# Seven of ten column blocks of the modulation vectors move from the projections to the hgrn heads and the output projection

## The chip, the cores and the metric

The kernel runs on one core of a Trainium2 chip. The metric is device time in microseconds (us) for one execution, the median of several; lower is better. The engines are PE (TensorE; PEld is its weight load), DVE (VectorE), ACT (ScalarE), POOL (GpSimd) and SP, which issues most DMAs. Each engine and each queue works through its instructions strictly in the order in which the program lists them.

## The reference

Two transformer blocks on 1024 tokens of width 1024, all in fp32. The places that bear on the change, cut:

```python
s_lat = jax.nn.silu(c);  s_ctx = jax.nn.silu(c_ctx)            # [1, 1024], [1024]
sh1, sc1, g1, sh2, sc2, g2 = jnp.split(s_lat @ ada_w + ada_b, 6)   # ada_w [1024, 6144]
h = modulate(rmsnorm(x, norm1_g), sh1, sc1);  p = h @ w_in
y_hy = hyena_mixer(p[..., :1536], ...)          # two long convolutions by FFT
y_hg, _ = hgrn_mixer(p[..., 1536:], pc, ...)    # 4 heads, two directions
x = x + g1 * (concat(y_hy, y_hg) @ w_out)
x = x + g2 * ec_moe(modulate(rmsnorm(x, norm2_g), sh2, sc2), ...)
...
# second block, layers 0 and 1, for the latent rows and for 256 context rows
shift, scale, gate = jnp.split(silu(c) @ w_mod[l] + b_mod[l], 3)   # w_mod[l] [1024, 3072]
```

The modulation vectors are the products `silu(c) @ ada_w`, `silu(c) @ w_mod[0]` and `silu(c) @ w_mod[1]`, each also for the context's `c_ctx`: 6, 3 and 3 blocks of 1024 columns. The first two blocks of `ada_w` are wanted at once. The other four are first wanted by the output projection (`g1`) and by the norm behind it (`sh2`, `sc2`), `w_mod[0]` by the second block's context stream, which starts beside the hgrn heads, and `w_mod[1]` by layer 1, a long time after.

## The kernel before

The program is written as pieces of work in a priority order, and a scheduler lays the instructions out on each engine. Tiles come from pools; a tile waits until the slot that it takes is released. The pieces, in order:

1. **Start**: the first two column blocks of `ada_w`, the norm, the transposed rows `T` as high and low halves.
2. **Projections and hyena side by side** (`interleave` in `build`): `hy_proj` and `hg_proj` multiply `T` with weights (`pp` tiles in PSUM, weights `ah`, `al`), while the hyena filters, their spectra and the long convolutions run (`pf` tiles). A third stream, `mods_rest`, lays ten column blocks of modulation vectors between them.
3. **hgrn** (`ctx_state`, `hgrn_head`, `ph` tiles), two heads in flight on tiles marked 0 and 1. Beside the heads stands the part of the second block's context stream that its input alone decides: `ctx_first` and `ctx_side` (`cp` and `cm` tiles, weights `wr` split into `wh` and `wl`). Its last eight pieces are the gate's, one per 128 channels: a 512 KB load, a split by ACT and POOL, 24 matmuls, one store to `dgc`.
4. **Output projection and routing** (`out_proj`: `pp`, `pi`, `pq` tiles, weights `wo`), then `topk` with `ctx_heads` (`cp` again), then the experts and the second block, which the change leaves as they are.

A column block is one step of `mod_rows`. It takes sixteen weight tiles of 128 rows and 512 columns, each with one matmul whose stationary side is the two columns of `silu` (a row of the order; fp32 is run in two passes, so the trace counts two matmuls). The sums lie in four strips of one PSUM tile `mp`. Two bias rows are loaded, four DVE additions (`mr<-mr,mp`) finish the block, and it is stored. After the last block of a group `rows_to_cols` loads part of it back, transposes it on PE and copies it out on ACT.

Of the kernel before, what the change touches and what calls it, by code (L numbers as in the profile page):

```python
# [22 lines left out]
D = 1024  # L23
# [107 lines left out]
class Kern:  # L131
# [11 lines left out]
    # ------------------------------------------------------------ storage  # L143
# [26 lines left out]
    def cst(self, shape, dt=F32, name="c"):  # L170
        return self.pc.tile(list(shape), dt, name=self.nm(name))
# [7 lines left out]
    # ------------------------------------------------------------ operations  # L179
# [73 lines left out]
    def columns(self):  # L253
        """the small vectors, 128 channels to a column"""
# [44 lines left out]
    # ------------------------------------------------------------ modulation vectors  # L299
# [6 lines left out]
    def mod_rows(self, w, bias, c0, ncols, s, rows, pt, tmp, raw):  # L306
        """rows[:, c0:c0+ncols] (DRAM, one row per vector) = s^T w + bias, 1024 columns per step"""
        for b0 in range(c0, c0 + ncols, 1024):
            ps = self.ps(pt)
            for k in range(8):  # L310
                for cb in range(2):
                    r = self.t(raw, [128, 512])
                    self.dma(r, w[k * 128:k * 128 + 128, b0 + cb * 512:b0 + cb * 512 + 512])
                    p0 = 64 * (k % 2) + 32 * cb
                    self.mm(ps[p0:p0 + 2], s[:, k, :], r, k < 2, k > 5)
# [8 lines left out]
    def rows_to_cols(self, rows, c0, nblk, pt, tmp):  # L324
        """[128, 2, nblk]: column form of rows[:, c0:c0 + 128 nblk]"""
# [9 lines left out]
    def mods_rest(self, pt, tmp, raw):  # L335
        """the modulation vectors of block 2 and the rest of block 1's"""
        I = self.I
        oc, occ = self.offb["c_2"], self.offb["c_ctx_2"]
        s = self.silu_cols(self.cb[:, oc:oc + 8], self.cb[:, occ:occ + 8])
        self.m2 = self.dram([2, 2, 3 * D], name="m2")  # L340
        self.A_2, self.sh_2 = [], []
        on = self.offb["norm_g_2"]
        for l in range(2):
            yield from self.mod_rows(I["w_mod_2"][l], I["b_mod_2"][l], 0, 3 * D, s, self.m2[l], pt, tmp, raw)
            mods = self.rows_to_cols(self.m2[l], 0, 16, pt, tmp)
            A = self.cst([128, 2, 8], name="A")
            for i in range(2):
                self.stt(A[:, i], mods[:, i, 8:16], 1.0, self.cb[:, on + l * 8:on + l * 8 + 8], ADD, MUL)
            self.A_2.append(A)
            self.sh_2.append(mods[:, :, 0:8])  # L350
        yield from self.mod_rows(I["ada_w"][0], I["ada_b"][0], 2 * D, 4 * D, self.scol, self.ada, pt, tmp, raw)
# [6 lines left out]
    # ------------------------------------------------------------ norm + modulate + transpose  # L358
# [18 lines left out]
    def transpose_mod(self, xs, A, sh, pt, tmp, emit, dst=None):  # L377
        """for each block k of D: [128, len(xs)*128 tok] = A * x^T + sh"""
# [40 lines left out]
    def wunits(self, w, c0, nc_, eng=None):  # L419
        """columns c0 .. c0+nc_ of w in units of 512 columns of 128 rows: a list of (hi, lo)"""  # L420
# [3 lines left out]
    def proj(self, w, hT, t0, n, pt):  # L424
        """[128 channels, n tokens] in PSUM"""
# [22 lines left out]
    def filter_mlp(self):  # L448
        """self.hst [128, 1024]: hidden features (hi over lo), one column per lag"""
# [31 lines left out]
    def filter_time(self):  # L481
        """even and odd parts of the windowed two-sided filters to DRAM; self.finv: per channel 1/(norm0 norm1)"""
# [60 lines left out]
    def fwd_butterfly(self, xa, xb):  # L543
        """x_a (a=0..7) in xa, xb [128,4,256]; yields (r, y), y [128, 2, 256] = (sum x cos, sum x sin) of pi a r / 8"""
# [78 lines left out]
    def filter_spectra(self):  # L623
        """Hd[o][half][r]: [128 j, 2, 256] = (Re, -Im) of the unnormalised spectrum at 16 j + r"""
# [19 lines left out]
    # ------------------------------------------------------------ long convolution of one half (256 channels)  # L644
# [156 lines left out]
    def hy_proj(self):  # L801
        """short-convolved v, x1, x2 in [token, channel] form to DRAM; x2 carries the filters' norms"""
# [1278 lines left out]
```

## Time and profile before

| what | value |
|---|---|
| runs | 4019.2 us median of 3 (4012.77 to 4020.24) |
| the profiled execution, from its first to its last instruction | 4024.9 us |
| share of the span busy: PE, DVE, ACT, POOL | 92%, 72%, 57%, 32% |
| projections beside the hyena | 115 to 821 us |
| the last long convolution alone | 821 to 893 us on PE |
| hgrn heads and context | 893 to 1157 us |
| output projection | 1157 to 1273 us |
| routing, up to the first experts | 1273 to 1375 us |

The page gives no time of the profiled execution other than its span, which is 5.7 us above the median of the runs. A window's line gives each engine's busy time in that stretch with the number of instructions, then the granted TensorE clock as a share of full speed, the busy share of the 16 DMA engines and what they moved. A busy matmul time counts a matmul from its start to its modelled end; since the next one starts earlier, the distance from start to start is the price of one in a stream.

### The profile page before, as it was taken

Reading aid. Unit: us, or ns where it says so; the run is one execution under the profiler, and the core shown is the slowest. Engines: PE = TensorE matmul, PEld = TensorE weight load, DVE = VectorE, ACT = ScalarE, POOL = GpSimd, SP = SyncE. Lnnn points to the kernel's source line nnn. Section 1 sums busy time; section 2 is a strip of 40 time slices with the busy share of each in tenths; the row PEclk is TensorE's granted clock in tenths of the full one; section 3 lists DMA queues with packets and bytes.
Section 4 is the critical chain, followed back from the end, with each engine's and each line's share of the span. In section 5 each row is a group of like instructions: output and inputs, shape, how many; then the busy total and the mean of one; then the engine's idle time right before and its main releaser. Section 6 shows DMA issues by size and latency. Waiting matters only on the chain. (4 is left out here: it accounts for less than half of the span.)

```text
span 4024.9 us, 54977 instructions
## 1 busy us (share of the span) xinstructions
PE 3685.7 (92%) x18922; PEld 2946.4 (73%) x18922; DVE 2907.8 (72%) x4414; ACT 2310.5 (57%) x3763; POOL 1290.8 (32%) x940
## 2 busy tenths in 40 slices
PE   6999999976887889999999999979999899999989
PEld 2667666646876677778777777768788788878878
DVE  4587767789843788889888888855677744567772
ACT  4433432226534688678777777755566654466662
POOL 3455533336612322311112111001344610143461
PEclk7999999987988999999999999989999999999999
DMA  7778777772345689999999999951311144131133
GB/s 227 227 227 247 229 234 229 221 237 86 95 151 191 188 298 346 342 326 334 356 365 355 368 362 356 343 178 65 117 53 38 49 149 123 59 121 49 40 97 113
DMA packets 538592, 824.41 MB, mean 205 GB/s; under 512 B 39089, under 2 KB 242887, under 8 KB 538312
## 3 DMA queue, kind: packets, MB, share of 16 engines
q1 hardware_dynamic: 511240, 755.75, 55.2%
q0 software_dynamic: 26048, 64.09, 5.8%
q8 instruction: 149, 2.44, 0.3%
q10 hardware_dynamic: 1024, 1.06, 0.1%
q14 instruction: 131, 1.07, 0.1%
HBM read 712.65 MB, written 107.05 MB: 204 GB/s over the span
## 5 line engine op out<-in xcount | busy, mean ns | idle before, releaser
L187 DVE TENSOR_TENSOR el<-er,eh 128x1024 fp32r<-128x1024 f32 x763 | 946.5, 1289 | 114.9 <-ACT eh L184 108.0
L184 ACT ACTIVATE eh<-er 128x1024 fp32r<-128x1024 f32 x768 | 785.4, 1057 | 144.5 <-PE ea L206 93.2
L205 PE MATMUL ea<-el,xh 128*128 128x512 f32 x1024 | 417.5, 408 | 19.1 <-DVE el L187 16.9
L204 PE MATMUL ea<-eh,xh 128*128 128x512 f32 x1024 | 406.3, 400 | 2.5 <-ACT eh L184 2.5
L206 PE MATMUL ea<-eh,xh 128*128 128x512 f32 x1024 | 405.9, 396 | 0.0
L1277 POOL DMA_INDIRECT acc<-yo,idx x16 | 78.0, 4875 | 757.4 <-DVE yo L196 757.4
L1508 DVE TENSOR_SCALAR_CACHE_REDUCE E<-s,rq 128x512 f32<-128x512 f32 (+1 forms) x384 | 239.3, 656 | 48.3 <-PE s L209 32.6
L205 PEld LDWEIGHTS ea<-el,xh 128*128 128x128 f32 x1024 | 193.7, 189 | 86.4 <-DVE el L187 45.3
L181 ACT ACTIVATE E<-E,a 128x1280 f32<-128x1280 f32 x160 | 216.5, 1359 | 53.5 <-DVE a L1512 49.0
L204 PEld LDWEIGHTS ea<-eh,xh 128*128 128x128 f32 x1024 | 193.9, 189 | 49.4 <-ACT eh L184 3.8
L209 PE MATMUL s<-KA,QA 128*128 128x512 f32 (+1 forms) x768 | 202.8, 388 | 27.8 <-DVE E L1508 27.7
L206 PEld LDWEIGHTS ea<-eh,xh 128*128 128x128 f32 x1024 | 194.0, 189 | 39.6
L205 PE MATMUL ey<-el,hh 128*128 128x512 f32 x512 | 205.4, 401 | 5.2 <-DVE el L187 5.2
L204 PE MATMUL ey<-eh,hh 128*128 128x512 f32 x512 | 203.8, 403 | 4.2 <-ACT eh L184 4.2
L209 PE MATMUL mp<-mr,silu 128*2 128x512 f32 x384 | 188.0, 643 | 21.5 <-DMA mr<-in_ada_w_dram 14.1
L206 PE MATMUL ey<-eh,hh 128*128 128x512 f32 x512 | 202.2, 395 | 0.0
L209 PE MATMUL pt<-dg,E 128*128 128x128 f32 x1280 | 184.1, 290 | 10.0 <-DVE a L1515 4.1
L184 ACT ACTIVATE u<-pp 32x512 f32<-32x512 f32 (+2 forms) x212 | 124.2, 586 | 103.8 <-PE pp L206 97.1
L209 PEld LDWEIGHTS pt<-dg,E 128*128 128x128 f32 x1280 | 170.8, 205 | 15.1 <-issue 9.7
L204 PE MATMUL pp<-T,ah 128*128 128x512 f32 x448 | 180.5, 403 | 0.0
L205 PE MATMUL pp<-T,ah 128*128 128x512 f32 x448 | 179.0, 400 | 0.0
L209 PEld LDWEIGHTS s<-KA,QA 128*128 128x128 f32 x768 | 133.2, 201 | 61.8 <-DVE E L1508 44.2
(527 smaller groups left out, 10043.4 us busy)
## 6 DMA issues: line engine op xcount, KB each, us to landing
er<-in_exp_w_dram SPq DMA_DIRECT2D x768, 512.0 KB
wr<-in_w_in_dram SPq DMA_DIRECT2D x60, 512.0 KB
dc<-in_k_dft_dram POOLq DMA_DIRECT2D x72, 384.0 KB, 4.6
mr<-in_ada_w_dram SPq DMA_DIRECT2D x96, 256.0 KB
mr<-in_w_mod_dram SPq DMA_DIRECT2D x96, 256.0 KB
dc<-in_k_dft_dram POOLq DMA_DIRECT2D x72, 256.0 KB, 4.5
ar<-in_w_in_dram SPq DMA_DIRECT2D x64, 256.0 KB
wr<-in_w_out_dram SPq DMA_DIRECT2D x24, 512.0 KB
```

The source lines that it names most:

```text
L181: return self.nc.scalar.activation(out, in_, func, **kw)
L184: return self.nc.scalar.activation(out, in_, AF.Copy)
L187: return (eng or self.nc.vector).tensor_tensor(out, a, b, op=op)
L204: mm(out, lh, rh, start=first, stop=False)
L205: mm(out, lh, rl, start=False, stop=False)
L206: mm(out, ll, rh, start=False, stop=last)
L209: self.nc.tensor.matmul(out, l, r, start=first, stop=last)
L1277: nc.gpsimd.indirect_dma_start(out=self.acc, out_offset=x[0], in_=yo, in_offset=None, compute_op=ADD)
L1508: nc.vector.tensor_scalar(E[:, k0:k1], o, r, None, op0=MUL, op1=ALU.min, accum_out=mx[:, m, j:j + 1] if nc_ > 1 else mc)
```

## The change

`mods_rest` is cut in three. `mods_layer(0)` (three blocks of `w_mod[0]`) stays beside the projections. `mods_tail` (four blocks of `ada_w`) now stands behind the heads in the program and ahead of `ctx_first`; `mods_layer(1)` (three blocks) stands behind `ctx_side`. The moved blocks load 1024 columns at a time, so each load is 512 KB in place of 256 KB and there are 56 loads in place of 112. They share the two `wr` slots with `ctx_side` and have one slot `mr` beside, and they put their sums into the one `cm` bank that the context stream uses too. Loads, matmuls, additions and stores of a block are otherwise the same. The rest of the diff renames the class, drops comments and docstrings, and runs the same program through `run`.

```diff
-    def mod_rows(self, w, bias, c0, ncols, s, rows, pt, tmp, raw):
+    def mod_rows(self, w, bias, c0, ncols, s, rows, pt, tmp, raw, wide=512):
...
                 for cb in range(2):
-                    r = self.t(raw, [128, 512])
-                    self.dma(r, w[k * 128:k * 128 + 128, b0 + cb * 512:b0 + cb * 512 + 512])
+                    if cb * 512 % wide == 0:
+                        r = self.t(raw[k % len(raw)] if wide > 512 else raw, [128, wide])
+                        self.dma(r, w[k * 128:k * 128 + 128, b0 + cb * 512:b0 + cb * 512 + wide])
                     p0 = 64 * (k % 2) + 32 * cb
-                    self.mm(ps[p0:p0 + 2], s[:, k, :], r, k < 2, k > 5)
+                    self.mm(ps[p0:p0 + 2], s[:, k, :], r[:, cb * 512 % wide:cb * 512 % wide + 512], k < 2, k > 5)
...
+        K.mods_first()
...
-                       (0, 11, [(K.mods_rest("mp", "mr", "mr"), 1)]))
+                   (0, 4, [(K.mods_layer(0, "mp", "mr", "mr"), 1)]))
...
             with ExitStack() as e2:
                 K.open_ps(e2, "right", cp=1, cm=1)
+                K.open(e2, "right", mr=1)
+                for _ in K.mods_tail("cm", "cv", ("wr", "wr", "mr"), 1024):
+                    pass
                 K.ctx_first()
                 K.ctx_side()
+                for _ in K.mods_layer(1, "cm", "cv", ("wr", "wr", "mr"), 1024):
+                    pass
```

How the scheduler lays this out on PE, at the three places that matter. First the end of the projections, before: `pp` rows are the projections, `mp<-mr,silu` rows the modulation vectors, `pf` the last long convolution.

```order
L204 MATMUL pp_8394<-T_402,ah_8361 128x512
L205 MATMUL pp_8394<-T_410,ah_8361 128x512
L206 MATMUL pp_8394<-T_402,al_8362 128x512
L209 MATMUL mp_6943<-mr_6986,silu_127 2x512
L209 MATMUL mp_6943<-mr_6989,silu_127 2x512
L204 MATMUL pf_7351<-yh_7343,dc_7347 128x256
L204 MATMUL pf_7429<-yh_7421,dc_7425 128x256
```

The same place with the change:

```order
L204 MATMUL pp_7962<-T_402,ah_7929 128x512
L205 MATMUL pp_7962<-T_410,ah_7929 128x512
L206 MATMUL pp_7962<-T_402,al_7930 128x512
L204 MATMUL pf_6987<-yh_6979,dc_6983 128x256
L204 MATMUL pf_7065<-yh_7057,dc_7061 128x256
```

Counted as the program lists them (the trace shows each as two passes), 142 of this stage's 160 modulation matmuls stood ahead of the last projection matmul and 18 among the 192 matmuls of the last long convolution. With the change 48 are left, all in the first half of the projections. The second place is the first head, before: `ph` rows are hgrn, `cp` and `cm` the context stream.

```order
L209 MATMUL ph_2215_8693<-hi_2205_8672,hi_2210_8682 128x128 x4
L212 MATMUL ph_2193_8636<-ident_116,hw_2184_8587 128x128 x2
L212 MATMUL cm_10291<-ident_116,cu_10286 128x4
L212 MATMUL cp_10340<-ident_116,cx_10319 128x128
L209 MATMUL ph_2218_8707<-hm_2217_8702,hm_2216_8701 128x128 x4
L209 MATMUL ph_2221_8719<-hm_2220_8714,hm_2219_8713 128x128 x4
```

With the change:

```order
L209 MATMUL ph_2074_8261<-hi_2064_8240,hi_2069_8250 128x128 x4
L209 MATMUL cm_9826<-wr_9827,silu_127 2x512 x2
L212 MATMUL ph_2052_8204<-ident_116,hw_2043_8155 128x128 x2
L209 MATMUL cm_9826<-wr_9831,silu_127 2x512 x2
L209 MATMUL cm_9826<-mr_9835,silu_127 2x512 x2
L209 MATMUL ph_2077_8275<-hm_2076_8270,hm_2075_8269 128x128 x4
L209 MATMUL ph_2080_8287<-hm_2079_8282,hm_2078_8281 128x128 x4
```

All 64 matmuls of `mods_tail` now stand between hgrn matmuls, most of them in the heads' first half, and the context's `cp` matmuls come later: before, all 312 stood ahead of the last hgrn matmul, now 192 do, 48 stand between it and the first `pp` matmul of the output projection, and 72 among the `pp` matmuls. There, the third place, PE had only the output projection's own `pp`, `pi` and `pq` matmuls before:

```order
L204 MATMUL pp_11107<-wo_11018,yt_11029 128x512
L212 MATMUL pi_11077<-ident_116,m_2814_11073 128x128 x4
L205 MATMUL pp_11107<-wo_11019,yt_11029 128x512
L206 MATMUL pp_11107<-wo_11018,yt_11031 128x512
L206 MATMUL pp_11135<-wo_10988,yt_11030 128x512
```

With the change:

```order
L206 MATMUL cp_10645<-Tc_10068,wl_10642 128x256
L209 MATMUL cm_10673<-wr_10678,silu_986 2x512 x2
L209 MATMUL cm_10673<-mr_10682,silu_986 2x512 x2
L212 MATMUL pi_10983<-ident_116,m_2762_10979 128x128 x4
L205 MATMUL pp_10999<-wo_10911,yt_10921 128x512
L206 MATMUL pp_10999<-wo_10910,yt_10923 128x512
```

The 48 matmuls of `mods_layer(1)` stand among the 384 `pp` matmuls of the output projection. On SP their loads stand between the loads of the output projection's own operands.

## Rows read from the trace of the kernel before

**Rows 1.** The page's part 1: engine, busy us, share, instructions.

```profile
PE 3685.7 (92%) x18922; PEld 2946.4 (73%) x18922; DVE 2907.8 (72%) x4414; ACT 2310.5 (57%) x3763; POOL 1290.8 (32%) x940
```

**Rows 2.** Windows over the five stretches, all instructions.

```profile
core 0: us, PE busy (x) PEld busy (x) DVE busy (x) ACT busy (x) POOL busy (x), PEclk, DMA share, GB/s
115.00:821.00 706.00, 687.36 (x3289) 469.14 (x3289) 508.65 (x806) 244.39 (x507) 324.28 (x302) 0.99 0.75 231
821.00:893.00 72.00, 51.39 (x230) 31.10 (x226) 61.96 (x126) 19.90 (x37) 22.90 (x36) 0.81 0.74 239
893.00:1157.00 264.00, 196.84 (x1417) 186.85 (x1417) 222.49 (x354) 145.56 (x373) 147.18 (x105) 0.84 0.33 103
1157.00:1273.00 116.00, 108.63 (x547) 91.45 (x548) 39.30 (x71) 49.56 (x118) 19.65 (x15) 0.95 0.43 147
```

**Rows 3.** PE's waits from 115 to 821 us, the three longest.

```profile
PE pf L204 <- ACT yh L184: 5.8, 2, 3.5
PE pp L212 <- DVE u L196: 5.6, 3, 2.3
PE mp L209 <- DMA mr<-in_w_mod_dram: 4.2, 5, 1.2
```

**Rows 4.** The first two windows, instructions of the tile mp alone (PE, PEld, DVE, ACT).

```profile
115.00:821.00 706.00, 142.63 (x288) 12.31 (x290) 21.77 (x32) 0.39 (x2) 0.99 0.75 231
821.00:893.00 72.00, 18.92 (x36) 1.38 (x32) 4.08 (x6) 0.00 (x0) 0.81 0.74 239
```

**Rows 5.** PE in order of time, late in the projections: start us, us, instruction.

```profile
802.77 0.39 PE L206 MATMUL pp<-T,al 128*128 128x512 f32 x1
803.00 0.39 PE L204 MATMUL pp<-T,ah 128*128 128x512 f32 x1
803.23 0.40 PE L205 MATMUL pp<-T,ah 128*128 128x512 f32 x1
803.56 1.02 PE L209 MATMUL mp<-mr,silu 128*2 128x512 f32 x2
804.51 0.50 PE L206 MATMUL pp<-T,al 128*128 128x512 f32 x1
804.85 0.39 PE L204 MATMUL pp<-T,ah 128*128 128x512 f32 x1
```

**Rows 6.** Two windows within the projections, all instructions.

```profile
250.00:300.00 50.00, 47.98 (x218) 32.33 (x216) 43.01 (x63) 21.07 (x46) 29.80 (x29) 1.00 0.74 218
700.00:750.00 50.00, 50.00 (x207) 31.29 (x206) 42.79 (x67) 14.36 (x28) 29.18 (x18) 1.00 0.76 246
```

**Rows 7.** PE's longest wait for the loads from 821 to 893 us, then PE in order of time.

```profile
PE mp L209 <- DMA mr<-in_ada_w_dram: 4.9, 6, 1.3
896.37 0.31 PE L212 MATMUL mp<-ident,mr 32*128 32x32 f32 x1 [4.02 <-DVE mr L187]
900.54 0.80 PE L209 MATMUL ph<-hw,h 128*128 128x128 f32 x2 [3.86 <-DMA hw<-dVc]
```

**Rows 8.** SP's queue in order of time, same place.

```profile
893.78 0.78 SPq L177 DMA_DIRECT2D mr<-ada  x2
896.34 0.23 SPq L177 DMA_DIRECT2D ada<-mr  x1
896.62 0.38 SPq L177 DMA_DIRECT2D hw<-dVc  x1
```

**Rows 9.** Two windows within the hgrn heads, all instructions.

```profile
920.00:940.00 20.00, 6.30 (x27) 5.49 (x28) 18.16 (x33) 10.73 (x22) 12.78 (x9) 0.51 0.40 129
980.00:1000.00 20.00, 19.52 (x157) 18.81 (x157) 20.00 (x39) 15.70 (x43) 13.24 (x12) 0.98 0.13 39
```

**Rows 10.** The window of the heads, instructions of the tile cp alone.

```profile
893.00:1157.00 264.00, 52.22 (x320) 43.51 (x320) 2.12 (x4) 10.19 (x26) 0.84 0.33 103
```

**Rows 11.** SP's queue, three of the gate's eight stores (all: 1055.7 to 1127.9 us).

```profile
L177 SPq DMA_DIRECT2D dgc<-cu x8: 319/320/332, 1055.7 to 1127.9; - x8
1102.50 0.32 SPq L177 DMA_DIRECT2D dgc<-cu  x1
1107.57 0.32 SPq L177 DMA_DIRECT2D dgc<-cu  x1
1113.57 0.32 SPq L177 DMA_DIRECT2D dgc<-cu  x1
```

**Rows 12.** SP issues wo's raw tiles; ACT and PE wait at the output projection's start.

```profile
1152.75 3.26 SPq L177 DMA_DIRECT2D xm<-in_w_out_dram  x3
1156.67 1.06 ACT L184 ACTIVATE wo<-xm 128x1024 fp32r<-128x1024 f32 x1 [2.86 <-DMA xm<-in_w_out_dram]
1162.42 1.12 PE L212 MATMUL pi<-ident,m 128*128 128x128 f32 x4 [5.55 <-ACT u L181]
```

More of the change, by code (lines that the diff above doesn't have):

```diff
@@ L128 @@
 ALIAS = {"cpt": "cm", "cs": "cp", "cpo": "cp"}
-class Kern:
+class Work:
     def __init__(self, tc, I, out, dbg=None, stop=None):
@@ L333, in rows_to_cols, with mods_first, mods_layer, mods_tail @@
         return dst
-    def mods_rest(self, pt, tmp, raw):
-        I = self.I
+    def mods_first(self):
         oc, occ = self.offb["c_2"], self.offb["c_ctx_2"]
-        s = self.silu_cols(self.cb[:, oc:oc + 8], self.cb[:, occ:occ + 8])
+        self.scol2 = self.silu_cols(self.cb[:, oc:oc + 8], self.cb[:, occ:occ + 8])
         self.m2 = self.dram([2, 2, 3 * D], name="m2")
         self.A_2, self.sh_2 = [], []
+    def mods_layer(self, l, pt, tmp, raw, wide=512):
+        I = self.I
         on = self.offb["norm_g_2"]
[L343 to L351, printed above, removed]
+        yield from self.mod_rows(I["w_mod_2"][l], I["b_mod_2"][l], 0, 3 * D, self.scol2, self.m2[l], pt, tmp, raw, wide)
+        mods = self.rows_to_cols(self.m2[l], 0, 16, pt, tmp)
+        A = self.cst([128, 2, 8], name="A")
+        for i in range(2):
+            self.stt(A[:, i], mods[:, i, 8:16], 1.0, self.cb[:, on + l * 8:on + l * 8 + 8], ADD, MUL)
+        self.A_2.append(A)
+        self.sh_2.append(mods[:, :, 0:8])
+    def mods_tail(self, pt, tmp, raw, wide=512):
+        I = self.I
+        yield from self.mod_rows(I["ada_w"][0], I["ada_b"][0], 2 * D, 4 * D, self.scol, self.ada, pt, tmp, raw, wide)
         mods = self.rows_to_cols(self.ada, 3 * D, 16, pt, tmp)
@@ L1964, with side_by_side, run @@
 LAM_INIT = [0.8 - 0.6 * math.exp(-0.3 * i) for i in range(2)]
+def side_by_side(*streams):
+    todo = [[-lead / total, total, list(gens)] for lead, total, gens in streams]
+    while todo:
+        s = min(todo, key=lambda t: t[0])
+        g, w = s[2][0]
+        if next(g, todo) is todo:
+            s[2].pop(0)
+            if not s[2]:
+                todo.remove(s)
+        else:
+            s[0] += w / s[1]
+def run(K):
+    fst = ExitStack()
+    with ExitStack() as e1:
+        K.open(e1, "left", ar=3, ah=4, al=4)
+        K.open_ps(e1, "left", pp=3, mp=1)
+        K.open(e1, "left", u2=4, T=16)
+        K.open_ps(fst, "right", pf=4)
+        K.open(fst, "right", f4=7, fb=5, y=2, t=3, H=2)
+        with ExitStack() as e2:
+            K.open(e2, "right", cr=6, x=4, c=2, mr=8)
+            K.start()
+        K.open(fst, "right", yh=2, yl=2, ph=2, pl=2, dc=5, ri=7, ra=2, mr=2)
+        K.mods_first()
+        side_by_side((30, 450, [(K.filter_time(), 2.4), (K.filter_spectra(), 2.1), (K.hyena(), 5)]),
+                   (0, 64, [(K.hy_proj(), 1), (K.hg_proj(), 1)]),
+                   (0, 4, [(K.mods_layer(0, "mp", "mr", "mr"), 1)]))
+    fst.close()
+    with ExitStack() as cx:
+        with ExitStack() as e1:
+            K.open_ps(e1, "left", ph0=3, ph1=3)
+            K.open(e1, "left", hmk=1, hS=2)
+            for p in "01":
+                K.open(e1, "left", **{"hi" + p: 6, "hw" + p: 5, "h2" + p: 3, "hm" + p: 4, "hT1" + p: 2, "hT2" + p: 4})
+            K.ctx_state()
+            for h in range(4):
+                K.hgrn_head(h)
+            K.open(cx, "right", wr=2, wh=2, wl=2, cu=6, cv=2, Tc=4, lg=2)
+            K.pfx = "c"
+            with ExitStack() as e2:
+                K.open_ps(e2, "right", cp=1, cm=1)
+                K.open(e2, "right", mr=1)
+                for _ in K.mods_tail("cm", "cv", ("wr", "wr", "mr"), 1024):
+                    pass
+                K.ctx_first()
+                K.ctx_side()
+                for _ in K.mods_layer(1, "cm", "cv", ("wr", "wr", "mr"), 1024):
+                    pass
+        K.open_ps(cx, "right", cp=1, cm=1)
+        K.pfx = "o"
+        em = cx.enter_context(ExitStack())
+        with ExitStack() as e0:
+            K.open_ps(e0, "left", pp=3, pq=2, pi=1)
+            with ExitStack() as e1:
+                K.open(e1, "left", xm=3, rw=1, wo=16, m4=3, yt=6, u2=3)
+                K.out_proj()
+            K.open(em, "left", el=4, eh=4, er=10)
+            with ExitStack() as e1:
+                K.open(e1, "left", twr=2, twh=2, twl=2)
+                K.open(e1, "left", aff=1, tk=12, tp=2, af=4)
+                K.topk()
+                K.pfx = "c"
+                K.ctx_heads("tw")
+        with ExitStack() as e1:
+            K.open_ps(e1, "left", et=1, ea=3, ey=2)
+            K.open(e1, "right", g2b=1, xg=1, xf=1, xh=4, sa=4, hh=4, yo=2)
+            side_by_side((0, 64, [(K.moe(), 1)]), (CL, CT, [(K.ctx_rest(), 1)]))
+    K.pfx = ""
+    with ExitStack() as e1, ExitStack() as e0, ExitStack() as ec:
+        K.open(e0, "right", T0=16)
+        rope = K.lat_pools(ec)
+        hT = K.first_rows()
+        K.lat_path(hT, rope, ec, e0, e1)
@@ L1968, with __init__, cst, start @@
+class Kern:
+    def __init__(self, tc, I, out, dbg=None, stop=None):
+        self.work = Work(tc, I, out, dbg, stop)
+        self.nc = tc.nc
+    def cst(self, shape, dt=F32, name="c"):
+        return self.pc.tile(list(shape), dt, name=self.work.nm(name))
+    def start(self):
+        W = self.work
+        W.pc, W.psm, W.pd, W.one = self.pc, self.psm, self.pd, self.one
+        run(W)
+    def __getattr__(self, name):
+        return lambda *a, **k: iter(())
 _INS = ['x', 'c', 'ctx', 'c_ctx', 'ada_w', 'ada_b', 'norm1_g', 'w_in', 'hy_conv_w', 'hy_conv_b', 'hy_pos_w1', 'hy_pos_b1',
```

## The prediction

> **What bounds the kernel now.** The page's part 1 says only that PE is busy 92% of the span [rows 1], an average over stages, so I read windows cut at the stages [rows 2]. From 115 to 821 us PE is busy 687 of 706 us at a granted clock of 0.99; DVE is at 509 (72%), the DMA engines at 0.75. A busy matmul time overlaps the next one, so two more views are wanted. PE's waits in this stretch are short, the longest three groups together 15.6 us [rows 3], and in order of time the projection's matmuls start every 0.23 us though each lasts 0.39 [rows 5]: PE issues without a gap. This stage ends when PE has done its list. From 821 to 893 us the last long convolution runs alone, PE busy 51 of 72 us and DVE 62: a chain between PE, ACT and DVE, not PE's work, sets that time. In the heads, 893 to 1157 us, PE is busy 197 of 264 us and DVE 222 [rows 2]; in some 20 us windows DVE has no idle time at all, in others PE is nearly empty, at half the clock [rows 9]. The output projection, 1157 to 1273 us, is PE's again: 109 of 116.
>
> So the change takes work from a stage that PE bounds, into one with 67 us of idle PE, and into a second one with hardly any. PE's total stays the same: all that can be won is idle time of PE that gets filled.
>
> **Term 1, the projections.** By the program's lists 94 modulation matmuls (142 less 48) leave the stretch ahead of the last projection matmul. The price of one: the tile's 288 passes took 142.6 us [rows 4], 0.495 us a pass, 0.99 us for the two passes of a matmul. In order of time it is more: from the projection matmul at 803.23 to the one at 804.85 are 1.62 us with one modulation matmul between them; without it the two steps from start to start would take 0.46, so its price is 1.16 us [rows 5], since the matmul behind it starts late too. 94 of them are 93 to 109 us, and I take 109 as PE's own relief. Not all of it comes back. DVE loses little, about six of the eight blocks' additions here, 24 x 0.68 = 16 us (21.8 us are 32 of them) [rows 4]. On average it goes to 493 of 597 us, 83%, still below PE. But the load is uneven: in 250 to 300 and 700 to 750 us DVE has 43 of 50 us [rows 6], and about ten modulation matmuls stand in 50 us (144 in 706 [rows 4]). Ten fewer would bring PE to 38 in the second slice, below the 40 that DVE has left when it gives up one block's additions (2.7 us). Such slices cost some 2 to 4 us each, and the two streams that are left then wait on one another more often than now. I take 95 us saved, between 70 (a third of the relief lost to such waits) and 109 (none lost).
>
> The loads leave with them: 94 x 256 KB are 24.6 MB of the 163 MB that 231 GB/s bring in 706 us, 15%, as the time also falls by 13%. So the DMA share stays near 0.75 and sets nothing.
>
> **Term 2, the last long convolution.** 18 modulation matmuls stood here, 18.9 us of PE [rows 4], mostly in idle time. But they stood in order: PE waited 4.9 us for their loads, then 4.0 us for DVE to finish the last block, and SP issued the load `hw<-dVc` only at 896.6 us, behind that block's round trip through DRAM (`ada<-mr`, `mr<-ada`); the first hgrn matmuls waited 3.9 us for it [rows 7, 8]. With the 18 gone these 12.8 us are free, but the convolution's own chain is next and ends hardly earlier. I take 8 us saved, between 0 and 13.
>
> **Term 3, the heads.** In come 64 modulation matmuls. Two now share a load and stand side by side, so I price them between 0.99 and 1.16, at 1.05: 67 us. Out go 120 of the 312 `cp` matmuls, at 52.2 us for 320 [rows 10] 0.163 each, 20 us. PE has 47 us more to do in a stretch with 67 us idle [rows 2]. If all of it fits into idle time the stretch does not grow, if none does it grows by 47. Against a full fit: DVE sets part of this stage, gets 16 additions of 0.68 (11 us), and the idle time lies in pieces between dependent steps. For it: much of the idle time is where the new matmuls stand, in the first half (13.7 of 20 us in 920 to 940, at a clock of 0.51 [rows 9]). I take 20 us more, between 0 and 47.
>
> **Term 4, the output projection.** In come 48 modulation matmuls at 1.05 (50 us) and the 120 `cp` matmuls (20 us). Idle PE here is 7.4 us [rows 2], and the first projection matmuls wait for ACT, 5.6 us, and behind a weight load that SP had not issued before 1152.75 [rows 12]: the 48 `cp` matmuls fall into that pause and cost little. 70 less 10 are 60 us. The 120 `cp` matmuls are five gate pieces; the fastest three stores of such pieces are 5.1 and 6.0 us apart [rows 11], so their own chain of load, split and matmuls could take 27 us in place of 20. I keep 60, between 52 (all pauses filled) and 70.
>
> DVE's twelve additions (8 us) lie in its idle time: it has 39 of 116 us busy here [rows 2]. Were that cover gone they would cost 8 us. Routing and experts follow the output projection by the same lists as before and move with it; the second block takes nothing from the moved blocks before it has long been stored. I cost all of that at nothing.
>
> **The sum.** -95 - 8 + 20 + 60 = -23 us. It is made on the profiled execution of 4024.9 us, which gives 4001.9; the median of the runs lies 5.7 us lower, at 4019.2, so I predict 3996. By the bounds of the four terms alone it could be from -70 (-109 - 13 + 0 + 52) to +47 (-70 + 0 + 47 + 70). What a measurement of this kernel can tell from no change is about 0.2%, 8 us.
>
> **The rivals.**
>
> *More is won.* All of the relief comes back and the heads take the new matmuls into idle time: -109 - 10 + 3 + 55 = -61, 3958 us. For it: PE's waits in the projections are so short [rows 3]. Against: DVE's slices at 43 of 50 [rows 6] and at 20 of 20 [rows 9].
>
> *The work is only moved.* The relief is 85, the heads use little of their idle time and grow by 35, the output projection by 60, the chain of the convolution gives 5: +5, within 8 us of before, 4024. For it: the heads' waits are on ACT and DVE steps in a chain, and PE in order puts about 2 us of modulation before a step that is ready. Against: the `cp` matmuls stood in the same gaps in groups of 20 to 24, 3 to 4 us at 0.163.
>
> *Slower: the moved matmuls wait for their loads.* PE in order waits at a modulation matmul whose load is late, and behind it stand hgrn or output projection matmuls. There are 56 wide loads, three slots, and a new load waits for PE to release a slot, on an SP queue that in between waits for slots of the heads' tiles. In the last long convolution six such waits took 4.9 us, 0.8 each [rows 7]. At 0.8 for each of the 56 loads it is 45 us: -23 + 45 = +22, 4041 us. The kernel is slower by over 8 us from 0.55 us a load on (31 us over 56). For it: a load of 512 KB has twice the bytes to land before its matmuls can start, and it stands in a queue behind other waits. Against: the DMA engines are busy 0.33 in the heads and 0.43 in the output projection, where it was 0.74 in that convolution [rows 2], and the projections with their two slots lost only 4.2 us to five waits [rows 3].
>
> *Slower: DVE bounds the projections.* If PE's busy time hides slack, the stage is bound by the engine with the next largest share, DVE, which gives back only the 16 us of its own additions: -16 - 8 + 20 + 60 = +56, 4075 us. The trace speaks against it: PE starts a matmul every 0.23 us without a gap [rows 5], while DVE stands idle 197 of 706 us [rows 2]. The Trainium skill's page "Perfetto Trace Analysis", section "Identifying the Most-Contended Engine", bears on this one: a matmul's busy share is no good measure because matmuls are pipelined, and the busy share of the weight loads should be read in its place. By that reading PE is at 66% here (469 of 706 us of PEld) and DVE, at 72%, is the most contended engine. The rule is about distance from the peak, and the starts without a gap say that PE is nevertheless what this stage waits for, so I give it little.
>
> **How the numbers follow.** My forecast, a gain of 8 to 45 us: 0.45. More won (beyond 45): 0.18. Only moved: 0.16. Late loads: 0.17. DVE: 0.04. Faster by over 0.2% is then 0.63, within it 0.16, slower 0.21. The range reaches from 3954, a little beyond the larger gain, to 4034, which takes in the moved case and the smaller half of the late loads, and leaves out about 0.08 below, the largest gains, and 0.12 above, the rest of the late loads and DVE. The likeliest case's own range is 3974 to 4011.
>
> **What would show it.** Right: the last projection matmul ends near 726 us with DVE busier than 80% before it; the last matmul of the long convolution near 790; the heads end near 1074 with PE busier than 85% in them; the output projection's last matmul is near 1250. Wrong: waits of PE for `wr` or `mr` loads of more than 30 us in all; PE waits of many tens of us on ACT or DVE in the projections; a stretch of heads longer than 300 us; or a changed time behind the routing, which I cost at nothing.

## The result, and the profile after

The changed kernel takes 3950.6 us (median of 4 runs, 3944.3 to 3952.2) against 4016.2 for the kernel before on the same chip (4 runs, 4012.8 to 4020.2): a ratio of 0.9827, 95% interval 0.9803 to 0.9851, 1.7% faster. A second set of runs gave 0.9821 (0.9799 to 0.9843). Forecast were 3996 us and a range of 3954 to 4034: the sign was right, the gain nearly three times the one forecast, and the time lies below the range.

The page's part 1 after, which answers to [rows 1]:

```profile
PE 3602.6 (91%) x18922; PEld 2940.1 (74%) x18922; DVE 2909.2 (74%) x4414; ACT 2305.5 (58%) x3757; POOL 1293.6 (33%) x940
```

As many PE instructions as before, and 83 us less PE time. That alone contradicts the prediction, which has "PE's total stays the same".

Windows of the changed kernel over the same stages as [rows 2] (projections, last long convolution, heads, output projection), then from the router's last logits to the last expert matmul, and from there to the last output store:

```profile
core 0: us, PE busy (x) PEld busy (x) DVE busy (x) ACT busy (x) POOL busy (x), PEclk, DMA share, GB/s
115.00:741.00 626.00, 583.89 (x3094) 467.57 (x3093) 489.04 (x779) 239.15 (x489) 331.09 (x300) 0.96 0.71 216
741.00:811.00 70.00, 36.19 (x195) 32.68 (x194) 66.11 (x123) 23.39 (x52) 30.04 (x37) 0.71 0.65 205
811.00:1078.00 267.00, 209.56 (x1454) 173.56 (x1452) 222.37 (x368) 139.14 (x362) 136.13 (x102) 0.87 0.47 154
1078.00:1224.00 146.00, 142.55 (x742) 103.35 (x741) 53.40 (x85) 56.54 (x129) 31.58 (x20) 0.99 0.68 227
1243.10:2557.20 1314.10, 1257.65 (x5845) 1009.74 (x5845) 1156.27 (x1131) 986.09 (x1220) 255.80 (x114) 0.99 0.96 336
2557.20:3946.70 1389.50, 1288.51 (x7234) 1104.70 (x7232) 864.37 (x1829) 794.37 (x1363) 461.08 (x309) 0.96 0.28 90
```

The last two stretches in the kernel before, cut at the same events:

```profile
1292.50:2618.00 1325.50, 1259.91 (x5845) 1011.21 (x5845) 1147.85 (x1131) 991.64 (x1224) 267.12 (x114) 0.98 0.95 333
2618.00:4021.00 1403.00, 1294.58 (x7234) 1108.40 (x7232) 870.85 (x1829) 793.77 (x1363) 462.40 (x309) 0.96 0.27 89
```

Stage by stage, before to after: the projections are 79 us shorter, the last long convolution 1.5, the heads 1.4 longer, the output projection 30 longer (116.1 to 146.4 us, heads' last store to the first expert weight load). So at that point the changed kernel leads by 49 us, not by 23. Then come two gains that the prediction has nowhere: 11 us from the router to the last expert, and 13.5 us in the second block. The instruction counts of PE in these two lines are the same as before, 5845 and 7234. (The kernel before starts its first expert matmul at 1364 us, and not at 1375 as the table of its stages has it.)

The first surprise shows in the modulation matmuls alone (the tile `silu`; columns PE, PEld, ACT), 115 to 1300 us of before, then of after, then after by stage:

```profile
115.00:1300.00 1185.00, 161.06 (x320) 13.42 (x320) 0.00 (x0) 0.93 0.63 197
```

```profile
115.00:1300.00 1185.00, 92.60 (x320) 8.40 (x320) 0.00 (x0) 0.91 0.65 203
115.00:741.00 626.00, 42.14 (x96) 3.28 (x96) 0.00 (x0) 0.96 0.71 216
811.00:1078.00 267.00, 29.21 (x128) 2.94 (x128) 0.00 (x0) 0.87 0.47 154
1078.00:1224.00 146.00, 21.24 (x96) 2.18 (x96) 0.00 (x0) 0.99 0.68 227
```

The 48 matmuls (96 passes) that stay beside the projections cost 0.88 us each; the 112 that moved cost 50.5 us in all, 0.45 each, though the prediction priced them at 1.05. In order of time one pair of them in the output projection reads:

```profile
1120.64 0.39 PE L206 MATMUL pp<-wo,yt 128*128 128x512 f32 x1
1120.86 0.39 PE L204 MATMUL pp<-wo,yt 128*128 128x512 f32 x1
1121.18 1.03 PE L209 MATMUL cm<-wr,silu 128*2 128x512 f32 x4
1122.14 0.50 PE L205 MATMUL pp<-wo,yt 128*128 128x512 f32 x1
```

Four passes, two whole matmuls, in 1.03 us, where before two passes, one matmul, took 1.02 [rows 5].

### The profile page after: what moved, and what is told of

Same layout as the page of the kernel before. It is cut to its first block, busy times and chain, and to the rows that moved or that the text cites. A ratio compares the mean times of both kernels' runs of the same rounds, so it can differ in the third digit from the quotient of the medians.

```text
span 3950.4 us, 54906 instructions
## 1 busy us (share of the span) xinstructions
PE 3602.6 (91%) x18922; PEld 2940.1 (74%) x18922; DVE 2909.2 (74%) x4414; ACT 2305.5 (58%) x3757; POOL 1293.6 (33%) x940
## 3 DMA queue, kind: packets, MB, share of 16 engines
q10 hardware_dynamic: 1024, 1.06, 0.2%
## 5 line engine op out<-in xcount | busy, mean ns | idle before, releaser
L206 PE MATMUL pp<-T,al 128*128 128x512 f32 x448 | 177.3, 396 | 0.0
L187 POOL TENSOR_TENSOR wl<-wr,wh 128x1024 fp32r<-128x1024 f32 (+1 forms) x48 | 117.6, 2459 | 179.2 <-ACT wh L184 177.8
```

Of the source, the lines that this page charges most:

```text
L187: return (eng or self.nc.vector).tensor_tensor(out, a, b, op=op)
L206: mm(out, ll, rh, start=False, stop=last)
```

## The experiments

Theory A: the two matmuls of one wide load stand next to each other on PE and write different 32-row strips of the PSUM tile (`p0 = 64*(k%2) + 32*cb`), and so take the time of one. Rivals: the place alone makes the gain (B); the wide load or the shared weights do (C). For the second surprise, theory O: the stages behind the router go by the order in which their instructions stand, which a change far ahead of them rearranges; rivals are the spread between executions, and a link to the moved blocks.

All kernels in one table, in us from the start of the profiled span: ends of the projections, the last long convolution, the heads and the router's logits (by the start of the last instruction of each); lengths of the experts (first to last expert matmul) and of the second block (to the last output store); PE time of the modulation matmuls from 115 to 1300 us; and the ratio to the kernel before.

| kernel | proj. | conv. | heads | router | experts | 2nd block | modul. | ratio (95%) |
|---|---|---|---|---|---|---|---|---|
| before | 821 | 892 | 1157 | 1293 | 1254 | 1403 | 161 | 1 |
| before, again (e0) | 815 | 888 | 1153 | 1288 | 1250 | 1403 | 161 | one run, 4020.1 us |
| changed | 741 | 811 | 1078 | 1243 | 1236 | 1390 | 93 | 0.9827 (0.9803–0.9851) |
| changed, again (a1) | 741 | 813 | 1077 | 1242 | 1239 | 1390 | 91 | 0.9821 (0.9799–0.9843) |
| e1 moved, narrow | 736 | 806 | 1062 | 1250 | 1256 | 1407 | 127 | 0.9947 (0.9933–0.9961) |
| e2 wide in place | 773 | 835 | 1100 | 1235 | 1258 | 1412 | 82 | 0.9910 (0.9896–0.9925) |
| e3 one strip | 743 | 815 | 1094 | 1277 | 1258 | 1401 | 146 | 0.9969 (0.9960–0.9979) |
| e4 all wide, moved | 726 | 798 | 1061 | 1224 | 1256 | 1404 | 72 | 0.9851 (0.9827–0.9875) |
| e5 four strips, moved | 726 | 812 | 1083 | 1242 | 1237 | 1406 | 56 | 0.9864 (0.9843–0.9884) |
| e6 four strips in place | 790 | 851 | 1113 | 1246 | 1257 | 1411 | 59 | 0.9911 (0.9892–0.9930) |
| e7 two steps later | 777 | 847 | 1175 | 1312 | 1240 | 1394 | 154 | 1.0003 (0.9991–1.0016) |
| e9 wide in place, sooner | 794 | 858 | 1119 | 1254 | 1239 | 1392 | 88 | 0.9862 (0.9841–0.9883) |
| e10 e4, order of changed | 722 | 794 | 1060 | 1227 | 1240 | 1388 | 70 | 0.9816 (0.9797–0.9834) |
| e11 e4, mixed order | 727 | 801 | 1065 | 1226 | 1240 | 1404 | 70 | 0.9826 (0.9813–0.9840) |

**e0 and a1, the two kernels once more.**

> The kernel before, once more, for a second trace of it. If the 18 us that the experts and the 14 us that the second block lost after the change are only the spread between two executions, this trace has them too against the first trace of before: experts and second block shorter by 10 us or more, no change anywhere else. If they belong to the change, every stage here is within 5 us of the first trace.

> The changed kernel once more, on the chip of the next two. The experts and the second block took 1236 and 1389 us in its first trace, against 1250 to 1258 and 1401 to 1412 us in the traces of before and of the three variants. If that belongs to its order of instructions, both come out within 4 us of 1236 and 1389 again and the time is 3951 us within 6; if it was the chip or the execution, they come out near 1252 and 1403 and the time near 3980 us.

Behind the router each came out at its first trace's lengths once more: experts 1250 and 1239 us, second block 1403.3 and 1390.0. One kernel's second block repeats within 1 us, its experts within 4. So the 13.5 us there, and most of what the experts lost, are no spread between executions; they belong to the program. Ahead of the router e0's projections ran 6 us shorter than in the first trace, one more than e0's text allows, so a difference of that size there is not told apart from spread.

**e1, the moved blocks with narrow loads.** Edit, on the changed kernel:

```diff
-                        r = self.t(raw[k % len(raw)] if wide > 512 else raw, [128, wide])
+                        r = self.t(raw[(2 * k + cb) % len(raw)] if isinstance(raw, tuple) else raw, [128, wide])
...
-                for _ in K.mods_tail("cm", "cv", ("wr", "wr", "mr"), 1024):
+                for _ in K.mods_tail("cm", "cv", ("wr", "wr", "mr"), 512):
```

(and the same for `mods_layer(1)`).

> The changed kernel with the seven moved blocks loaded 512 columns at a time again: only the place moves. Theory A (neighbours): two modulation matmuls that stand next to each other on TensorE and write different 32-row strips of PSUM take the time of one; a lone one costs 0.92 us, a group about 0.95 us. With narrow loads the order of TensorE has the 112 moved matmuls in some 70 groups (44 of them alone), so about 66 us in place of the 54 us measured in the changed kernel: about 3963 us (3955 to 3975). Rival B (the place alone, idle TensorE filled): as the changed kernel, 3951 us within 6. The prediction's own prices (1.05 us for each moved matmul): 3996 us.

Measured 3999.9 us. B is out: the place without the wide loads is worth 0.5%, not 1.7%. A was short: PE has 34 us more modulation time than in the changed kernel where 12 were expected (the moved matmuls of the changed kernel, 54 us in this forecast, take 50.5 in the windows above); why it is so much is open. And most of the loss does not show where the matmuls stand: at the router's end e1 is only 7 us behind. The rest comes behind it: 28 us up to the last expert, for which the last modulation matmuls, now as late as 1257 us, are one possible cause, and 18 in the second block, which has the work of the changed kernel. That it lands on the prediction's 3996 is a coincidence of sums: its heads are 9 us shorter than before, where 20 longer were forecast.

**e2, wide loads in place.** Edit, on the kernel before: the `wide` of the change's `mod_rows`, and

```diff
-            yield from self.mod_rows(I["w_mod_2"][l], I["b_mod_2"][l], 0, 3 * D, s, self.m2[l], pt, tmp, raw)
+            yield from self.mod_rows(I["w_mod_2"][l], I["b_mod_2"][l], 0, 3 * D, s, self.m2[l], pt, tmp, raw, 1024)
...
-            K.open(e1, "left", u2=4, T=16)
+            K.open(e1, "left", u2=3, T=16)
```

> The kernel before with all ten blocks left beside the projections, only their loads made 1024 columns wide (two buffers of 4 KB; one of the four u2 buffers is given up for them). Theory A: about 150 groups of modulation matmuls become about 80 of 0.95 us, 60 us less TensorE work in a stretch that TensorE bounds: about 3955 us (3945 to 3975), as fast as the changed kernel without any move. Rival B (the place makes the gain): 4016 us within 8, slower if the lost u2 buffer matters.

3984.4 us, above A's 3955 and far from B's 4016. Ahead of the router A holds: modulation time falls from 161 to 82 us, and the router ends at 1235, 8 us sooner than in the changed kernel, with nothing moved. The forecast of 3955 is missed behind it: experts 1258 and second block 1412.

**e3, one strip.** Edit, on the changed kernel, for the wide blocks:

```diff
-                    p0 = 64 * (k % 2) + 32 * cb
-                    self.mm(ps[p0:p0 + 2], s[:, k, :], r[:, cb * 512 % wide:cb * 512 % wide + 512], k < 2, k > 5)
+                    p0 = 64 * (k % 2) + 32 * cb if wide == 512 else 0
+                    first, last = (k < 2, k > 5) if wide == 512 else (k + cb == 0, k + cb == 8)
+                    self.mm(ps[p0:p0 + 2], s[:, k, :], r[:, cb * 512 % wide:cb * 512 % wide + 512], first, last)
...
```

> The changed kernel, same loads, same places, the two matmuls of a load still next to each other and with the same weights, but all of them write the first strip of the PSUM tile and the additions read that strip alone, so the modulation vectors hold sums of both column halves. Theory A: no two can run side by side, 112 matmuls at 0.92 us are 103 us in place of 54: 20 to 49 us longer, 3970 to 4000 us, by how much of it idle time of TensorE takes up. Rival C (the gain comes from shared weights or from the wide load itself): 3951 us within 6, price 0.45 us a matmul as in the changed kernel.

4009.3 us, 9 above the range. PE in order of time, the same kind of pair as above, and the window of the output projection that it stands in:

```profile
1151.97 0.40 PE L206 MATMUL pp<-wo,yt 128*128 128x512 f32 x1
1152.30 1.88 PE L209 MATMUL cm<-wr,silu 128*2 128x512 f32 x4
1154.11 0.50 PE L204 MATMUL pp<-wo,yt 128*128 128x512 f32 x1
```

```profile
1094.00:1257.00 163.00, 160.87 (x715) 103.41 (x714) 50.19 (x84) 54.25 (x126) 28.80 (x19) 1.00 0.61 199
```

1.88 us in place of 1.03, with the same load, the same weights and the same neighbours: only the strip differs. It is not a slower clock either: 1.00 was granted here, 0.99 in the changed kernel's output projection, and the `pp` matmuls around both pairs take the same time. That both add to the same address is not the cost by what the projection's matmuls show: they do so too, three in a row on one `pp` tile in the order ahead of the prediction, and start every 0.23 us [rows 5]. C is out, and A's price is shown. The modulation time rises by 53 us and the router ends 34 us later, inside A's 20 to 49, so idle time still takes up a third. The other 25 us, which A's range did not hold, lie behind the router again (experts 1258, second block 1401).

The Trainium skill, page "TensorEngine Tiling (Array Packing)", section "Tiling Modes", says that the array can be split into independent tiles, four of them at 128x32, and that "Different tiles can execute LdWeights and Matmul in parallel". The pair of the changed kernel beside that of e3 agrees for two tiles, 1.03 against 1.88 us; four come next.

**e5 and e6, four strips at a time.** The new function, used for all ten blocks, moved (e5) and in place (e6), with `u2=3`, cut:

```diff
...
+        for b0 in range(c0, c0 + ncols, 512):
+            ps = self.ps(pt)
+            for h in range(2):
+                for kk in range(2):
+                    r = self.t(raw[(2 * h + kk) % len(raw)], [128, 4, 256])
+                    self.dma(r, w[kk * 512:kk * 512 + 512, b0 + h * 256:b0 + h * 256 + 256].rearrange("(k p) n -> p k n", p=128))
+                    for j in range(4):
+                        self.mm(ps[32 * j:32 * j + 2, h * 256:h * 256 + 256], s[:, 4 * kk + j, :], r[:, j, :], kk == 0, kk == 1)
...
```

> The changed kernel with every moved block and the three that stay loaded as four row blocks by 256 columns, so that the four matmuls of a load write the four strips and stand next to each other (in the order of TensorE nearly all groups are of four or more; 20 additions more on VectorE, one u2 buffer given up for the second 4 KB buffer). Theory A carried on, four strips side by side: a group of four 256-column matmuls takes about 0.5 us, so 112 moved matmuls' work falls from 54 to about 28 us and that of the 48 beside the projections from 44 to about 14: with TensorE the bound about 3895 us (3885 to 3925). Rival D, only two strips run side by side: the moved ones stay at 54 us, those beside the projections fall to about 24: 3930 us within 10.

> The kernel before, all ten blocks in their place beside the projections, but with the same loads of four row blocks by 256 columns. Theory A with four strips side by side: 160 matmuls' work falls from about 140 us, or 75 us with loads 1024 wide in place (3984 us), to about 42: 3950 us (3935 to 3970), so that the move would then be worth what e5 lies below it. Rival D, two at a time: as the 1024-wide loads in place, 3984 us within 10.

PE in order of time in e5:

```profile
1126.19 0.40 PE L206 MATMUL pp<-wo,yt 128*128 128x512 f32 x1
1126.52 0.61 PE L209 MATMUL cm<-wr,silu 128*2 128x256 f32 x8
1127.07 0.50 PE L204 MATMUL pp<-wo,yt 128*128 128x512 f32 x1
```

Four matmuls of 256 columns in 0.61 us: four strips do run side by side, and rival D is out as to the price. The modulation time falls to 56 and 59 us. The times do not follow: 3970.6 and 3991.8 us, slower than the changed kernel and than e2. In e5 the projections end 16 us sooner, the convolution behind them ends where it did, and the second block is 17 us longer. In e6 the projections end 17 us later than in e2, with less PE work. The PE waits that differ most, in e2, 115 to 773 us:

```profile
PE pf L205 <- DVE yl L187: 8.2, 8, 3.3
PE mp L209 <- DMA mr<-in_w_mod_dram: 1.9, 4, 0.6
PE mp L209 <- DMA mr<-in_ada_w_dram: 0.7, 1, 0.7
```

and in e6, 115 to 790 us:

```profile
PE pf L205 <- DVE yl L187: 17.2, 16, 2.8
PE mp L209 <- DMA mr<-in_w_mod_dram: 8.1, 8, 2.8
PE mp L209 <- DMA mr<-in_ada_w_dram: 6.1, 4, 2.3
```

Waits for DVE and for the loads grow by 20 us. DVE has 40 additions of 0.68 us more here (27 us), since four strips must be summed: four more in each of ten blocks, and not the 20 that the forecast for e5 names. PE is no longer what this stage waits for alone.

**e7 and e9, the same blocks in place at another pace.** Edits: e7 is the kernel before with the first line, e9 is e2 with the second.

```diff
-                       (0, 11, [(K.mods_rest("mp", "mr", "mr"), 1)]))
+                       (-2, 11, [(K.mods_rest("mp", "mr", "mr"), 1)]))
+                       (2, 11, [(K.mods_rest("mp", "mr", "mr"), 1)]))
```

> The kernel before, with narrow loads and every block in its place, only the modulation vectors two of their eleven steps later against the projections. The order of TensorE's instructions in the experts then becomes the one that the changed kernel and e5 have (5184 rows from the first to the last expert matmul, against 5208 to 5210 in before, e1, e2, e3 and e6). Theory O (the experts' time goes by the order in which the context's pieces lie among them, not by the moved blocks): the experts take 1236 us within 4, as in the changed kernel. Rival (it belongs to the moved blocks): 1252 us within 4. Ahead of the experts theory A gives some 25 us, since 94 in place of 142 modulation matmuls stand alone; the second block has an order of its own, 1389 to 1412 us: in all 3980 us within 15.

> The 1024-wide loads in place (e2, 3984 us) with the modulation vectors two of their eleven steps sooner. The work is that of e2; the order of TensorE in the experts and in the second block becomes that of the changed kernel but for a few rows. Theory O: experts 1236 us and second block 1390 us within 4 in place of 1258 and 1412, on e2's earlier start of the experts (1309 us): 3940 us (3930 to 3955), faster than the changed kernel with nothing moved. Rival: as e2, 3984 us within 8.

Behind the router both went as theory O said: experts 1240 and 1239 us, second block 1394 and 1392, without any block moved. So the gain there has no link to the moved blocks. Ahead of it both forecasts failed. In e7 the modulation matmuls now reach into the heads, to 941 us, and the heads end 18 us later; the gain behind is spent (4025.8 us, ratio 1.0003). In e9 the projections end at 794 in place of e2's 773, so it takes 3968.3 us and not 3940. PE is idle for 40 us of that stage, against 26 in e2, and 7 us longer busy; why the sooner pace does that was not tried.

**e4, e10 and e11, all ten blocks wide, in three orders.** e4 is the changed kernel with `mods_layer(0)` wide too and `u2=3`, e10 and e11 are e4 with other names in the rotation of buffers:

```diff
-                   (0, 4, [(K.mods_layer(0, "mp", "mr", "mr"), 1)]))
+                   (0, 4, [(K.mods_layer(0, "mp", "mr", ("mr",), 1024), 1)]))
...
-                for _ in K.mods_tail("cm", "cv", ("wr", "wr", "mr"), 1024):
+                for _ in K.mods_tail("cm", "cv", ("wr", "mr"), 1024):
...
-                for _ in K.mods_layer(1, "cm", "cv", ("wr", "wr", "mr"), 1024):
+                for _ in K.mods_layer(1, "cm", "cv", ("wr", "mr", "wr"), 1024):
```

(the last two edits are e10; e11 has `("mr", "wr", "wr")` in the last line).

> The changed kernel with 1024-wide loads for the three blocks that stay beside the projections too (one u2 buffer given up for the second 4 KB buffer). Theory A alone: some 15 to 20 us less of TensorE in the projections, about 3935 us. Theory O: the order of TensorE in the experts and the second block falls back to that of before, 1256 and 1403 us within 4, so 34 us are lost there and the time is about 3970 us (3960 to 3985), slower than the changed kernel with less work.

> The kernel with 1024-wide loads for all ten blocks and seven of them moved (e4, 3962 us), its work unchanged; only the buffers that the moved loads take in turn are named in another order, wr, mr for the first four and wr, mr, wr for the last three. By that TensorE's order in the experts becomes that of the changed kernel (95% of its rows) and in the second block the same row for row (over 99%). Theory O: experts 1238 us and second block 1390 us within 4, in place of the 1256 and 1404 us of e4, with some 10 us of the context's work ahead of the experts instead: 3940 us (3930 to 3948), faster than the changed kernel. Rival (the buffers change nothing): 3962 us within 6.

> As the run before it, the last three blocks' loads in the order mr, wr, wr: TensorE's order is that of the changed kernel in the experts, but that of the kernel before in the second block (over 99% of its rows). Theory O: experts 1238 us, second block 1403 us within 4, so 13 us over the run before it: 3953 us (3943 to 3960). Rival: both the same.

Measured 3962.1, 3942.3 and 3951.1 us: all three within their ranges by theory O, and each stage behind the router within 4 us of its forecast. The runs of e10 (3935 to 3960) and e11 (3949 to 3959) overlap, so it is the stage lengths in the traces that tell these two apart. Windows from the router's end to the last expert and on to the last store, of e4, e10 and e11:

```profile
1223.70:2549.80 1326.10, 1257.26 (x5845) 1006.79 (x5845) 1147.44 (x1131) 991.13 (x1223) 268.33 (x114) 0.99 0.96 332
2549.80:3953.80 1404.00, 1292.04 (x7234) 1105.87 (x7232) 872.00 (x1829) 794.02 (x1363) 464.14 (x309) 0.96 0.27 89
```

```profile
1226.90:2541.50 1314.60, 1253.14 (x5844) 1004.79 (x5845) 1153.09 (x1131) 986.11 (x1219) 255.58 (x114) 0.99 0.96 335
2541.50:3929.90 1388.40, 1285.25 (x7234) 1101.42 (x7232) 866.15 (x1829) 794.70 (x1363) 462.06 (x309) 0.96 0.28 90
```

```profile
1226.40:2540.70 1314.30, 1255.69 (x5845) 1007.73 (x5845) 1153.73 (x1131) 985.78 (x1219) 254.46 (x114) 0.99 0.96 336
2540.70:3944.70 1404.00, 1294.46 (x7234) 1109.62 (x7232) 872.08 (x1829) 794.23 (x1363) 463.06 (x309) 0.95 0.27 89
```

The same work, 11.5 us between two orders in the first line (e4 against e10 and e11) and 15.6 in the second (e11 against e10). Where they differ in the first: in e10 and e11 the last piece of the context's gate, 24 `cp<-Tc,twh` and `cp<-Tc,twl` matmuls, stands ahead of the first expert matmul, in e4 behind the first two. PE's wait that goes with it, in the kernel before:

```profile
PE cm L209 <- POOL cdg L192: 7.0, 2, 3.8
```

is 6.2 us in e4 and not among the waits of the changed kernel, e10 or e11. In the second block one group of waits goes with the order: before, changed, e10 and e11 read

```profile
PE po L205 <- DVE tl L187: 24.9, 16, 5.7
```

```profile
PE po L205 <- DVE tl L187: 18.9, 16, 4.2
```

```profile
PE po L205 <- DVE tl L187: 18.4, 16, 4.2
```

```profile
PE po L205 <- DVE tl L187: 24.8, 16, 5.8
```

That is 6 of the 13 to 16 us. The traces also hold the rest. The orders of e10 and e11 in the second block differ in one stretch alone, from about 370 to 600 us behind the last expert matmul; windows around it, cut at the same two matmuls, of e10 and then of e11:

```profile
2899.00:3205.30 306.30, 282.36 (x1704) 245.25 (x1703) 210.69 (x529) 194.64 (x315) 139.14 (x87) 0.97 0.23 75
```

```profile
2896.60:3218.30 321.70, 290.40 (x1704) 252.62 (x1703) 216.90 (x529) 194.27 (x316) 140.32 (x87) 0.94 0.21 71
```

Here lie 15.4 of the 15.6 us, for the same 1704 matmuls. PE is idle 7.4 us longer, 6.5 of them in the group above (7.5 and 14.0 us in these windows), and busy 8.0 us longer, at a granted clock of 0.94 in place of 0.97. By that ratio alone 282 us would become 291, an estimate from these two lines. The changed kernel has e10's order in this stretch and takes 308.5 and 308.7 us in its two traces; the kernel before has e11's and takes 320.0 and 319.6. In the first line the lead is as local: it changes only in the first 630 us behind the router and then stays at 11.4 to 11.5 us, between e4 and e10 as between before and changed. What it is made of, beyond the gate's wait, stays open.

e10 is the fastest kernel of all in its trace (3933.7 us, the changed kernel 3950.4). By the timed runs its ratio of 0.9816 lies inside the interval of the changed kernel's, so that it beats it is not shown.

## Why the prediction was wrong, point by point

**The bound was right.** Relief in the projections came back: PE loses 100 us of modulation time there (142.6 in [rows 4] to 42.1) and the stage 79. The rival that DVE bounds this stage (+56) fell, and with it, for this stage, the reading by the weight loads' busy share that the prediction weighed beside it: DVE is busy 20 us less (508.7 to 489.0) and the stage is 79 us shorter. **Term 1** (−95, 70 to 109) measured −79, in its bounds: PE's idle time rose from 19 us [rows 2] to 42, which is the loss to uneven slices that the term allowed for; the two longest waits are now on DVE and ACT. The granted clock of the stretch fell as well, from 0.99 to 0.96 (0.99 and 0.97 in the second traces), which the term did not have; what that cost is not separated here.

```profile
PE pf L205 <- DVE yl L187: 17.6, 11, 3.2
PE pf L204 <- ACT yh L184: 12.5, 4, 5.0
```

**Term 2** (−8, 0 to 13) measured −1.5: the convolution's own chain was next, as was feared; PE now waits 13.5 us in one piece for ACT's `yh`.

**Terms 3 and 4 failed, at their common price.** "Two now share a load and stand side by side, so I price them between 0.99 and 1.16, at 1.05": both bounds came from matmuls that stand alone, in [rows 4] nearly all of them and in [rows 5] the one shown. The moved 112 cost 0.45 each, 50 us in place of 117. The heads grew by 1.4 and not by 20 (inside its bounds), the output projection by 30 and not by 60 (outside 52 to 70). Together that is 48 us better than forecast; with the 25 of the next point, less the 22 that terms 1 and 2 promised too much, it makes the 51 us by which the profiled execution's gain of 74 exceeds the 23. e3 shows that the strip makes the price, and how much of the 48 us that is: with the pairs in one strip the heads grow by 13 and the output projection by 48, so the pairing is worth 29. Of the other 19, some 11 would come from the price of a moved matmul in e3 (0.95 against 1.05, times 112; an estimate); the rest no run separates. The strips could be read in `mod_rows`, and the text itself says "side by side", but no bound was taken for matmuls that overlap. The trace of the kernel before had one to offer: nine times two modulation matmuls stand together there, five of these pairs taking 1.03 us. One is the pair at the end of the projections that the order ahead of the prediction shows:

```profile
820.56 0.39 PE L206 MATMUL pp<-T,al 128*128 128x512 f32 x1
820.88 1.03 PE L209 MATMUL mp<-mr,silu 128*2 128x512 f32 x4
```

"More won" (3958) is the nearest rival by its time, and not by its cause: the relief did not all come back.

**"I cost all of that at nothing" failed.** Routing, experts and second block gave 25 us: 11.4 and 13.5. The work is the same there, but not the order of the instructions, and e4, e10 and e11 show that the order alone makes steps of this size. The text names a changed time behind the routing as a mark of being wrong, yet the range holds nothing for it.

**The other marks.** Projections 741 (726 forecast), convolution 811 (790), heads 1078 (1074), output projection 1224 (1250). DVE is busy 78% in the projections (over 80 was said), PE 78% in the heads (over 85): the cheaper matmuls leave it idle. Late loads: PE waits 9.1 us for `wr` loads from 741 us on, 4 times, not the 45 of that rival.

```profile
PE cm L209 <- DMA wr<-in_ada_w_dram: 9.1, 4, 5.1
```

**What the change is worth by parts.** Up to the router's end, wide loads without the move (e2) gain 58 us, the move without wide loads (e1) 43, both 49, both and the remaining three blocks wide (e4) 69; a second trace of the kernel before ends its router 4 us sooner, so a few us between these say nothing. Up to there, then, wide loads alone gain as much as the changed kernel, with nothing moved. The changed kernel's last 25 us are its luck with the order.

## What to carry to other kernels

When an edit changes which instructions are neighbours, price them as neighbours: look for a place in the trace where two of them already stand together, and take that as one end of the bound, above all when they have as few output rows as here. Where a scheduler sets the order, a change early in the program rearranges stages that it does not touch: compare the orders of those stages before costing them at nothing, widen the range by what other orders cost (here 24 us between the fastest and the slowest of the twelve kernels in a 1400 us stage of equal work), and read an experiment's effect at the end of the stage it touches, not from the total.

## What was not expected of the hardware

Two matmuls with two output rows each, in neighbouring strips, take 1.03 us where one after the other in one strip takes 1.88, and four of 256 columns take 0.61. The order effect is as exact as a change of work: a second block of 1390 us repeated within 1 us in a second trace, one of 1403 us likewise.
